# Two transformer blocks on one core: where the down factors of a hidden pair are split, and how the conditioning rows are summed

## The chip, the core and the metric

The kernel runs on one core of one Trainium2 chip. The metric is the device time of the whole program in microseconds (us). Three runs of the kernel before gave 2796.27, 2797.93 and 2798.13 us, median 2797.93.

The engines that matter: TensorE (PE in the profile; PEld is its weight load), VectorE (DVE), ScalarE (ACT), GpSimd (POOL) and SyncE (SP). ACT and SP also issue DMAs; those rows read ACTq and SPq.

## The reference

Two layers run one after the other on a 1024 x 1024 activation (1024 tokens, model width 1024), all in fp32. The first is a hybrid mixer (gated MLP, differential attention, top-k attention) with layer norm, the second is conditioned on a vector `c` and mixes by stick-breaking attention and pooling. Each ends in the same kind of feed-forward part with 2816 hidden units. What the change touches is this:

```python
# layer 1, feed-forward
gate, up = jnp.split(x @ w_gu, 2)                       # 2 x (1024 x 2816)
x = layer_norm(alpha * x + (silu(gate) * up) @ w_down)
# layer 2, conditioning rows (shift, gain and scale), 6 x 1024 numbers
mod = jax.nn.silu(c) @ w_cond + b_cond
# layer 2, feed-forward
f = (jax.nn.silu(h @ w_gate) * (h @ w_up)) @ w_down
```

## The kernel before

**Matmuls.** An fp32 product is made of three matmuls on rounded parts (`mm3`, lines 97 to 99): each operand is split into a high part, a cast by ACT to the type fp32r (`split`, line 80), and a low part, what the cast left over, by DVE (line 84). A matmul has 128 x 128 weights and 512 columns.

**Feed-forward parts** (called FFN1 and FFN2 here). The 22 hidden tiles are taken in 11 pairs by `gate_up`. Pairs 0 and 1 are multiplied directly. Each pair from 2 to 10 uses a Strassen-Winograd scheme: seven products for the gate and seven for up, in the order 1, 6, 2, 7, 5, 4, 3, each of 12 matmuls, so 168 to a pair. G7 stands here for gate product 7 and U3 for up product 3. In names of the trace the activation operand tells the product: B11 is 1, T2 is 6, B21 is 2, T3 is 7, T1 is 5, T4 or B12 is 4, B22 is 3; `x1` in front is FFN1, `x3` is FFN2.

`product` (line 940) takes a slot of the tag "w" (a `wst` tile), casts the weights' high part into it on ACT (line 945), makes the low part on DVE, or on POOL for products 2 and 4 (line 946), issues the matmuls and then adds the result up in `after`: line 958 copies product 1, 963 is product 6, 983 the silu of product 2 of the gate, 966 product 7, 968 product 5, 971 product 4, 976 product 3; line 985 is the silu of the other gate parts, 992 and 994 multiply gate and up (994 on POOL).

**Down factors.** A finished pair is four 128 x 512 quarters (a11, a12, a21, a22: two hidden tiles by two halves of the tokens). The down projection needs seven factors of them: A11, A12, A22, and four sums, S1 = a21 + a22, S3 = a11 - a21, S2 = S1 - a11, S4 = a12 - S2. `forms` (line 1034) is a generator that makes one factor a step: the sum on DVE (lines 1044, 1047, 1050, 1059), then `store`, which takes another slot of the tag "w" (an `hf` tile), splits into it and puts the 512 KB DMA to DRAM off until the next store (`flush`, line 1023, on ACT's queue). The last two pairs, 9 and 10, store four plain quarters instead. `wst` and `hf` tiles share six slots, so a cast may have to wait until the store of an earlier `hf` has landed.

Before the change `gate_up` makes `todo = forms(p, ...)` after all 14 products of pair p, and steps it once after each product of the next pair's gate.

**Conditioning.** `cond_steps(j)` (line 1260) makes conditioning row j of six during FFN1: for each of eight blocks of `w_cond`, a 512 KB load `raw_c` on SP's queue (line 1265) and one DVE operation that scales it and adds it to `mod` (1267, 1269), then the bias, a split with a two-matmul column sum per half (1284) and a gain. `extra1` steps it after every second product of a Strassen pair.

**Order.** The whole program is written in one stream; a scheduler of the framework then sets each engine's order from modelled times, and `soon()` (high priority) pulls splits and evictions forward. At run time each engine goes through its list in that order, and an instruction that waits holds up all behind it on that engine.

Of the kernel before, what the change touches and what calls it, by code (L numbers as in the profile page):

```python
# [9 lines left out]
F32 = mybir.dt.float32  # L10
# [6 lines left out]
OP = mybir.AluOpType  # L17
# [5 lines left out]
D = 1024  # L23
P = 128
NB = S // P
KT = D // P
# [12 lines left out]
def two_blocks(ctx: ExitStack, tc: tile.TileContext, a):  # L39
    nc = tc.nc  # L40
    V, A, T, G, DMA = nc.vector, nc.scalar, nc.tensor, nc.gpsimd, nc.sync
# [14 lines left out]
    def slot(tag, shape, dtype, name):  # L56
        return strm.tile(shape, dtype, tag=tag, bufs=SLOTS[tag], name=name)
# [57 lines left out]
    def row(t, src):  # L115
        DMA.dma_start(t, src.partition_broadcast(P))
        return t
# [22 lines left out]
    for i, (k0, nk) in enumerate(((0, 3), (3, 3), (6, 2))):  # L140
        h, l = load_split(a["wu0"][:, k0:k0 + nk, :], [P, nk, U0N], hi_eng="dve", lo_eng="pool")
# [66 lines left out]
    for h, l, k0, nk in wu0:  # L208
        for j in range(nk):
            k = k0 + j  # L210
# [258 lines left out]
    for blk in SCORED:  # L469
        L = (blk + 1) * P  # L470
        nch, n = key_chunks(L)
# [10 lines left out]
        for h in range(8):  # L482
# [3 lines left out]
            r = p1.tile([P, S], F32, name="r", **GT)  # L486
# [164 lines left out]
    accp, _ = pool("accp", "right")  # L651
# [249 lines left out]
    NPAIR = (NFT - NLAST) // 2  # L901
    FORMS = ("A11", "S3", "S2", "A22", "S1", "A12", "S4")
    h_d = [{n: dr.tile([P, 2, 512], F32, name=f"h_d{i}{n}") for n in FORMS} for i in range(NPAIR)]
    hl_d = [dr.tile([P, 2, S], F32, name=f"hl_d{i}") for i in range(NLAST)]
# [91 lines left out]
    class Ffn:  # L996
# [36 lines left out]

        def forms(self, i, b):

            if i >= NPAIR:
                for (j, th), x in b.items():
                    self.store(hl_d[2 * (i - NPAIR) + j][:, :, th * 512:(th + 1) * 512], x)
                    yield
                return  # L1040
            a11, a12, a21, a22 = b[0, 0], b[1, 0], b[0, 1], b[1, 1]
            put = lambda n, x: self.store(h_d[i][n], x)
            s1 = self.post("s1")
            V.tensor_tensor(s1, a21, a22, op=OP.add)
            put("A11", a11)
            yield
            V.tensor_tensor(a21, a11, a21, op=OP.subtract)  # L1047
            put("S3", a21)
            yield
            V.tensor_tensor(a11, s1, a11, op=OP.subtract)  # L1050
            put("S2", a11)
            yield
            put("A22", a22)
            yield
            put("S1", s1)
            yield
            put("A12", a12)
            yield
            V.tensor_tensor(a12, a12, a11, op=OP.subtract)
            put("S4", a12)  # L1060
            yield

        def gate_up(self, wg, wu, late, extra=None):


            act = self.act

            def direct(f, th, g, u):
                pg = ps_lg()
                for n, (wh, wl) in enumerate((g, u)):  # L1070
                    for k in range(KT):
                        mm3(pg[:, n, :], wh[:, k, :], wl[:, k, :], act.at(0, k, th), act.at(1, k, th), k == 0, k == KT - 1)
                s = self.post("silu")
                with soon():
                    A.activation(s, pg[:, 0, :], AF.Silu)
                    V.tensor_tensor(s, s, pg[:, 1, :], op=OP.mult)
                return s

            def load(w, f):
                return load_split(w(f), [P, KT, P])  # L1080

            wt = [self.w0, [load(wg, 1), load(wu, 1)], [load(wg, 2)], []]
            b = {}
            for th in range(2):
                for f in range(2):
                    b[f, th] = direct(f, th, *wt[f])
                    if th == 0:
                        late(4 + 2 * f)
                        late(5 + 2 * f)
            todo = self.forms(0, b)  # L1090
            wt[2].append(load(wu, 2))
            wt[3].append(load(wg, 3))
            b = {}
            for th in range(2):
                b[0, th] = direct(2, th, *wt[2])
            wt[3].append(load(wu, 3))
            for th in range(2):
                for _ in range(4):
                    next(todo, None)
                b[1, th] = direct(3, th, *wt[3])  # L1100
            act.sums()
            todo = self.forms(1, b)
            for p in range(2, NFT // 2):
                f = 2 * p
                ms = {}
                for m in range(2):
                    w = (wg, wu)[m]
                    ms[m] = (Gate, Up)[m]([self.load(w(f + i), [P, KT, P]) for i in range(2)], act, self.post)
                    if m == 1:
                        ms[1].gate = ms[0]  # L1110
                    for q in (1, 6, 2, 7, 5, 4, 3):
                        ms[m].product(q)
                        next(todo, None)
                        if extra is not None:
                            extra()
                todo = self.forms(p, {(i, l): ms[0].p[i, l] for i in range(2) for l in range(2)})
            for _ in todo:
                pass
            self.flush()
# [129 lines left out]
    fpool, f_done = pool("fpool")  # L1249


    sc = fpool.tile([P, KT], F32, name="sc")
# [6 lines left out]

    def cond_steps(j):  # L1260

        m = fpool.tile([P, D], F32, tag="rows", bufs=1, name="mod")
        for k in range(KT):
            r = slot("raw", [P, D], F32, "raw_c")
            DMA.dma_start(r, a["w_cond_2"][k * P:(k + 1) * P, j * D:(j + 1) * D])
            if k == 0:
                V.tensor_scalar_mul(m, r, sc[:, 0:1])
            else:
                V.scalar_tensor_tensor(m, r, sc[:, k:k + 1], m, op0=OP.mult, op1=OP.add)
            yield  # L1270

        b = slot("raw", [P, D], F32, "raw_b")
        DMA.dma_start(b[0:1, :], a["b_cond_2"][j * D:(j + 1) * D].partition_broadcast(1))
        V.tensor_tensor(m[0:1, :], m[0:1, :], b[0:1, :], op=OP.add)
        gn = {1: "g_mix_pre_2", 2: "g_mix_post_2", 4: "g_ffn_pre_2", 5: "g_ffn_post_2"}.get(j)
        if gn is not None:
            g = row(slot("raw", [P, D], F32, "raw_g"), a[gn])
        for c in range(2):
            cs = slice(c * 512, (c + 1) * 512)
            hl = [ffn1.post(f"m{i}", F32R) for i in "hl"]  # L1280
            split(*hl, m[:, cs])
            o = ps_mm(512)
            for i in range(2):
                T.matmul(o, ones, hl[i], start=i == 0, stop=i == 1)
            V.tensor_copy(m[:, cs], o)
            yield
        if gn is not None:
            V.scalar_tensor_tensor(m, m, 1.0 if j in (1, 4) else 0.0, g, op0=OP.add, op1=OP.mult)
        DMA.dma_start(mod_d[j:j + 1, :], m[0:1, :])

    n_extra = [0]
# [1 line left out]

    def extra1():
        n_extra[0] += 1
        if n_extra[0] % 2 == 0:
            next(conds, None)

    tail = {}
# [339 lines left out]
    n = 0  # L1639
# [121 lines left out]
```

## Time and profile before

| what | value |
|---|---|
| median of 3 runs | 2797.93 us |
| the profiled execution's own time | 2798.06 us |
| its span, first to last instruction | 2796.3 us |
| mean granted TensorE clock | 0.935 of full |
| PE busy | 2436.5 us, 87% of the span |
| DVE, ACT, POOL busy | 65%, 39%, 28% |
| the chain that ended last | PE 48%, DVE 9%, DMA 7%, ACT 5%, POOL 4% |

The span and the times stand 1.8 us apart. FFN1's pairs lie from about 747 to 1257 us, FFN2's from about 2094 to 2565 us. Where the granted clock is 0.5, TensorE runs at 1.2 GHz rather than 2.4 GHz.

### The profile page before, as it was taken

The numbers are of one execution on the slowest core, as the hardware profiler recorded it, in microseconds if no ns is written. First come the engines' busy times: TensorE is split into PE (matmuls) and PEld (weight loads), VectorE is DVE, ScalarE is ACT, GpSimd is POOL, SyncE is SP. The second block draws the span as 40 slices with busy tenths as digits, with TensorE's granted clock in tenths as the row PEclk, the third lists the DMA queues.
The fourth block names the chain that finished last, engine by engine and source line by source line (L and its number), as shares of the span: only waits on it lengthen the run. The fifth ranks groups of instructions, "written<-read, shape, count | busy, mean of one in ns | idle before, by whom it ended". The sixth has DMA issues, their size and how long they took to land.

```text
span 2796.3 us, 32919 instructions
## 1 busy us (share of the span) xinstructions
PE 2436.5 (87%) x11584; PEld 1990.3 (71%) x11584; DVE 1825.5 (65%) x3042; ACT 1099.3 (39%) x2013; POOL 778.0 (28%) x751
## 2 busy tenths in 40 slices
PE   8889987998988777889997989898697887888998
PEld 8878776886766556668876777687576665666886
DVE  4889788468666677658775366757645545545776
ACT  4558954333232233223235344445723323324221
POOL 2511234136311121120034043428531111112004
PEclk9989998999999898999998999899798998999999
DMA  4244545422444455467733424644233323327663
GB/s 171 66 140 121 147 132 172 111 87 93 158 150 149 151 188 167 163 236 254 264 129 115 150 89 127 198 114 148 97 113 131 110 91 123 118 91 260 237 228 133
DMA packets 171726, 414.02 MB, mean 148 GB/s; under 512 B 21788, under 2 KB 67868, under 8 KB 170536
## 3 DMA queue, kind: packets, MB, share of 16 engines
q1 hardware_dynamic: 149064, 337.45, 37.6%
q10 hardware_dynamic: 22496, 74.46, 6.6%
q8 instruction: 92, 1.51, 0.2%
q14 instruction: 74, 0.61, 0.1%
HBM read 278.65 MB, written 133.19 MB: 147 GB/s over the span
## 4 chain that ended last, share of the span: by engine, by line
PE 48%; DVE 9%; DMA 7%; ACT 5%; POOL 4%; issue 3%; SPq 0%; ACTq 0%; DVEq 0%; POOLq 0%
PE plg L97 8%; PE plg L98 7%; PE plg L99 7%; PE pmm L97 5%; PE pmm L99 5%; PE pmm L98 5%; PE ptr L97 2%; PE ptr L99 2%; PE ptr L98 2%; ACT hf L80 2%; DMA raw_c<-in_w_cond_dram 1%; ACT wst L945 1%; POOL u L994 1%; PE plg L337 1%; DMA hl_d<-hf 1%
## 5 line engine op out<-in xcount | busy, mean ns | idle before, releaser
L946 POOL TENSOR_TENSOR wst<-rw,wst 128x512 fp32r<-128x512 f32 x57 | 82.0, 1438 | 327.0 <-ACT wst L945 263.1
L337 PE MATMUL plg<-qk,qk 128*128 128x384 f32 (+4 forms) x480 | 127.1, 383 | 30.0 <-DVE mn L350 15.0
L84 POOL TENSOR_TENSOR wl<-raw,wh 128x1024 fp32r<-128x1024 f32 (+2 forms) x28 | 66.3, 2373 | 304.9 <-ACT wh L80 278.5
L946 DVE TENSOR_TENSOR wst<-tt,wst 128x512 fp32r<-128x512 f32 x144 | 110.3, 767 | 36.7 <-ACT wst L945 36.5
L80 ACT CAST hf<-u 128x512 fp32r<-128x512 f32 x36 | 22.2, 616 | 275.1 <-DVE u L1047 222.9
L994 POOL TENSOR_TENSOR u<-u,u 128x512 f32<-128x512 f32 x36 | 47.3, 1314 | 293.1 <-DVE u L968 243.7
L945 ACT CAST wst<-tt 128x512 fp32r<-128x512 f32 x144 | 88.6, 617 | 81.2 <-PE plg L99 28.0
L1562 DVE TENSOR_TENSOR_SCAN sab<-sab 128x640 f32<-128x640 f32 (+7 forms) x64 | 103.2, 1617 | 22.0 <-ACT sab L1560 21.3
L278 ACT ACTIVATE junk_a<-xi,cand 128x1024 bf16<-128x1024 f32 (+1 forms) x124 | 109.0, 879 | 12.5 <-DVE cand L267 6.9
L337 PEld LDWEIGHTS plg<-qk,qk 128*128 128x128 f32 x480 | 83.6, 201 | 40.6 <-DVE mn L350 16.4
L80 ACT CAST ws<-st 128x512 fp32r<-128x512 f32 x72 | 45.0, 628 | 124.9 <-PE plg L99 77.1
L1188 DVE TENSOR_TENSOR dacc<-dacc,plg 128x1024 f32<-128x1024 f32 x48 | 58.5, 1219 | 53.2 <-PE plg L99 53.2
L162 PE MATMUL pmm<-wh,xh 128*128 128x256 f32 (+1 forms) x320 | 91.7, 287 | 1.3 <-DVE stgl L399 0.8
L163 PE MATMUL pmm<-wl,xh 128*128 128x256 f32 (+1 forms) x320 | 91.0, 285 | 0.0
L164 PE MATMUL pmm<-wh,xl 128*128 128x256 f32 (+1 forms) x320 | 90.8, 284 | 0.0
L351 ACT ACTIVATE e<-e,mn 128x128 f32<-128x128 f32 (+7 forms) x96 | 74.2, 773 | 37.2 <-DVE mn L350 35.9
L945 ACT CAST wst<-rw 128x512 fp32r<-128x512 f32 x86 | 53.1, 617 | 89.4 <-PE plg L99 31.3
L97 PE MATMUL pmm<-xh,wh 128*128 128x512 f32 x192 | 77.2, 402 | 7.4 <-DVE oB L585 4.8
L692 PE MATMUL pmm<-woh,mixh 128*128 128x512 f32 x192 | 78.9, 411 | 4.8 <-ACT mixh L681 2.6
L80 ACT CAST wh<-raw 128x1024 fp32r<-128x1024 f32 x54 | 56.6, 1049 | 67.2 <-PE pmm L98 28.8
L976 DVE TENSOR_TENSOR u<-plg,u 128x512 f32<-128x512 f32 x36 | 24.9, 691 | 86.2 <-PE plg L99 86.1
L971 DVE TENSOR_TENSOR p<-plg,u 128x512 f32<-128x512 f32 x36 | 24.8, 690 | 84.3 <-PE plg L99 84.2
(733 smaller groups left out, 8565.3 us busy)
## 6 DMA issues: line engine op xcount, KB each, us to landing
raw_c<-in_w_cond_dram SPq DMA_DIRECT2D x48, 512.0 KB, 4.6
qk<-qkd SPq DMA_DIRECT2D x72, 256.0 KB, 6.9
rw<-in_wgu_dram SPq DMA_DIRECT2D x36, 512.0 KB, 4.0
rw<-in_w_down_dram SPq DMA_DIRECT2D x26, 512.0 KB, 4.8
x_d<-acc SPq DMA_DIRECT2D x24, 512.0 KB, 2.9
qk<-qk2d SPq DMA_DIRECT2D x48, 256.0 KB, 4.2
raw<-in_wqk_dram SPq DMA_DIRECT2D x20, 512.0 KB, 4.8
raw<-in_w_down_dram SPq DMA_DIRECT2D x18, 512.0 KB, 4.5
```

The costliest lines, as they stand in the source:

```text
L80: A.copy(hi, src)
L97: T.matmul(out, lh, rh, start=start, stop=False, skip_group_check=more)
L98: T.matmul(out, lh, rl, start=False, stop=False, skip_group_check=more)
L99: T.matmul(out, ll, rh, start=False, stop=stop, skip_group_check=more)
L162: T.matmul(o, at(0, k, tb * P, P), h[:, j, :], start=(k == 0), stop=False)
L163: T.matmul(o, at(0, k, tb * P, P), l[:, j, :], start=False, stop=False)
L164: T.matmul(o, at(1, k, tb * P, P), h[:, j, :], start=False, stop=(k == KT - 1))
L278: A.activation(junk_a[:, :L], xi[self.blks[i]], AF.Sign, bias=c, accum_out=self.cnt[:, i:i + 1])
L337: T.matmul(pl[:, c, :n], q[:, isl], k2[:, c * n:(c + 1) * n], start=(j == 0), stop=last)
L945: A.copy(wh, x)
L946: (G if p in (2, 4) else V).tensor_tensor(wl, x, wh.bitcast(F32), op=OP.subtract)
L1562: V.tensor_tensor_scan(sa[:, ::-1], sa[:, ::-1], sa[:, ::-1], 1.0, op0=OP.mult, op1=OP.bypass)
```

## The change

Three things change. `forms` is made when five up products of a pair are still to come (before U5, whose quarter is not finished then), not after the last, and yields its factors in another order: those that need no sum first (A11, A22, A12, stepped after U5, U3 and the next pair's G1), then the sums (S3, S2, S1, S4, after G2, G7, G5 and G4), with two empty steps between. The plain pairs get the same kind of order, and the direct pairs take six steps rather than four per half. `cond_steps` now uses each load one step after it was issued, so that it has 13 steps to a row and not 10. The diff:

```diff
@@ -1033,28 +1033,33 @@
 
         def forms(self, i, b):
 
+
             if i >= NPAIR:
-                for (j, th), x in b.items():
-                    self.store(hl_d[2 * (i - NPAIR) + j][:, :, th * 512:(th + 1) * 512], x)
+                plain = lambda j, th: self.store(hl_d[2 * (i - NPAIR) + j][:, :, th * 512:(th + 1) * 512], b[j, th])
+                for n in ((0, 0), None, (1, 1), (1, 0), None, (0, 1)):
+                    if n:
+                        plain(*n)
                     yield
                 return
+            put = lambda n, x: self.store(h_d[i][n], x)
+            put("A11", b[0, 0])
+            yield
+            yield
+            put("A22", b[1, 1])
+            yield
+            put("A12", b[1, 0])
+            yield
+            yield
             a11, a12, a21, a22 = b[0, 0], b[1, 0], b[0, 1], b[1, 1]
-            put = lambda n, x: self.store(h_d[i][n], x)
             s1 = self.post("s1")
             V.tensor_tensor(s1, a21, a22, op=OP.add)
-            put("A11", a11)
-            yield
             V.tensor_tensor(a21, a11, a21, op=OP.subtract)
             put("S3", a21)
             yield
             V.tensor_tensor(a11, s1, a11, op=OP.subtract)
             put("S2", a11)
             yield
-            put("A22", a22)
-            yield
             put("S1", s1)
-            yield
-            put("A12", a12)
             yield
             V.tensor_tensor(a12, a12, a11, op=OP.subtract)
             put("S4", a12)
@@ -1095,7 +1100,7 @@
                 b[0, th] = direct(2, th, *wt[2])
             wt[3].append(load(wu, 3))
             for th in range(2):
-                for _ in range(4):
+                for _ in range(6):
                     next(todo, None)
                 b[1, th] = direct(3, th, *wt[3])
             act.sums()
@@ -1109,11 +1114,14 @@
                     if m == 1:
                         ms[1].gate = ms[0]
                     for q in (1, 6, 2, 7, 5, 4, 3):
+                        if m == 1 and q == 5:
+                            for _ in todo:
+                                pass
+                            todo = self.forms(p, ms[0].p)
                         ms[m].product(q)
                         next(todo, None)
                         if extra is not None:
                             extra()
-                todo = self.forms(p, {(i, l): ms[0].p[i, l] for i in range(2) for l in range(2)})
             for _ in todo:
                 pass
             self.flush()
@@ -1259,22 +1267,25 @@
 
     def cond_steps(j):
 
-        m = fpool.tile([P, D], F32, tag="rows", bufs=1, name="mod")
-        for k in range(KT):
-            r = slot("raw", [P, D], F32, "raw_c")
-            DMA.dma_start(r, a["w_cond_2"][k * P:(k + 1) * P, j * D:(j + 1) * D])
-            if k == 0:
-                V.tensor_scalar_mul(m, r, sc[:, 0:1])
-            else:
-                V.scalar_tensor_tensor(m, r, sc[:, k:k + 1], m, op0=OP.mult, op1=OP.add)
+        m, last = fpool.tile([P, D], F32, tag="rows", bufs=1, name="mod"), None
+        for k in range(KT + 1):
+            if k < KT:
+                r = slot("raw", [P, D], F32, "raw_c")
+                DMA.dma_start(r, a["w_cond_2"][k * P:(k + 1) * P, j * D:(j + 1) * D])
+            if k == 1:
+                V.tensor_scalar_mul(m, last, sc[:, 0:1])
+            elif k:
+                V.scalar_tensor_tensor(m, last, sc[:, k - 1:k], m, op0=OP.mult, op1=OP.add)
+            last = r
             yield
 
         b = slot("raw", [P, D], F32, "raw_b")
         DMA.dma_start(b[0:1, :], a["b_cond_2"][j * D:(j + 1) * D].partition_broadcast(1))
-        V.tensor_tensor(m[0:1, :], m[0:1, :], b[0:1, :], op=OP.add)
         gn = {1: "g_mix_pre_2", 2: "g_mix_post_2", 4: "g_ffn_pre_2", 5: "g_ffn_post_2"}.get(j)
         if gn is not None:
             g = row(slot("raw", [P, D], F32, "raw_g"), a[gn])
+        yield
+        V.tensor_tensor(m[0:1, :], m[0:1, :], b[0:1, :], op=OP.add)
         for c in range(2):
             cs = slice(c * 512, (c + 1) * 512)
             hl = [ffn1.post(f"m{i}", F32R) for i in "hl"]
@@ -1286,6 +1297,7 @@
             yield
         if gn is not None:
             V.scalar_tensor_tensor(m, m, 1.0 if j in (1, 4) else 0.0, g, op0=OP.add, op1=OP.mult)
+        yield
         DMA.dma_start(mod_d[j:j + 1, :], m[0:1, :])
 
     n_extra = [0]
@@ -1293,7 +1305,7 @@
 
     def extra1():
         n_extra[0] += 1
-        if n_extra[0] % 2 == 0:
+        if n_extra[0] % 4:
             next(conds, None)
 
     tail = {}
```

`extra1` steps the conditioning on three of four products, no longer on one of two.

How the scheduler's order changes is shown at two places. The numbers behind the names are running numbers of the tiles.

First, PE at the boundary between pairs 4 and 5 of FFN2, in the kernel before: the first matmul of each stretch of a product (`wst` is its weights).

```order
L99 MATMUL plg_18199<-x3B22h_16355,wst_18253 128x512
L97 MATMUL pmm_18276<-x3B21h_16352,wst_18327 128x512
...
L97 MATMUL plg_18349<-x3T3h_17286,wst_18350 128x512
...
L99 MATMUL pmm_18276<-x3B21h_16352,wst_18327 128x512
...
L99 MATMUL plg_18349<-x3T3h_17286,wst_18350 128x512
...
L97 MATMUL plg_18349<-x3T1h_16701,wst_18373 128x512
...
L97 MATMUL pmm_18443<-x3B11h_16350,wst_18444 128x512
```

The same place in the changed kernel:

```order
L99 MATMUL plg_18199<-x3B22h_16355,wst_18257 128x512
L97 MATMUL ptr_18306<-x3T2h_17293,wst_18307 128x512
...
L97 MATMUL pmm_18284<-x3B21h_16352,wst_18328 128x512
...
L97 MATMUL plg_18352<-x3T3h_17286,wst_18353 128x512
...
L97 MATMUL pmm_18443<-x3B11h_16350,wst_18444 128x512
...
L97 MATMUL plg_18352<-x3T1h_16701,wst_18377 128x512
...
L99 MATMUL pmm_18443<-x3B11h_16350,wst_18444 128x512
```

G6 (`x3T2`) now stands between U3 (`x3B22`) and G2 (`x3B21`), and before it stood ahead of U3; U1 (`x3B11`) has begun ahead of G5 (`x3T1`).

ACT there, before: `hf` casts are factors (u2 is S3, s11 is S2, u3 is A22, s1 is S1, p1 is A12), `wst` casts are weights (in order G2, G7, G5, G4), L1023 issues a store, L983 is the silu of G2.

```order
L80 CAST hf_18324<-u2_18020 128x512
L945 CAST wst_18327<-raw_18272 128x512
L80 CAST hf_18346<-s11_18042 128x512
L945 CAST wst_18350<-tt_18351 128x512
L80 CAST hf_18370<-u3_18067 128x512
L945 CAST wst_18373<-tt_18302 128x512
L1023 DMA h_d4S3_6143<-hf_18324 128x1024
L1023 DMA h_d4S2_6144<-hf_18346 128x1024
L1023 DMA h_d4A22_6145<-hf_18370 128x1024
L80 CAST hf_18391<-s1_18294 128x512
...
L945 CAST wst_18394<-rw_18274 128x512
L983 ACTIVATE s11_18342<-pmm_18276 128x512
```

ACT there in the changed kernel (the `hf` of u2 is S3, of s11 S2, of s1 S1 and of p1 S4; the `wst` rows are G2, G7, G5, G4 and last U1):

```order
L945 CAST wst_18328<-raw_18280 128x512
...
L983 ACTIVATE s11_18343<-pmm_18284 128x512
L80 CAST hf_18349<-u2_18026 128x512
L945 CAST wst_18353<-tt_18354 128x512
L80 CAST hf_18374<-s11_18043 128x512
L945 CAST wst_18377<-tt_18308 128x512
L80 CAST hf_18395<-s1_18345 128x512
L945 CAST wst_18398<-rw_18282 128x512
L1023 DMA h_d4S3_6143<-hf_18349 128x1024
L1023 DMA h_d4S2_6144<-hf_18374 128x1024
L80 CAST hf_18417<-p1_18000 128x512
...
L945 CAST wst_18444<-rw_18439 128x512
```

S3's cast stood directly ahead of G2's weight cast; now it stands behind the silu of G2 and ahead of G7's weight cast, and the stores of S3 and S2 are issued behind G4's cast and ahead of S4's.

Second, DVE in FFN1, where a block of conditioning steps lies. Before, around the end of pair 4 (L971 and L976 add up U4 and U3, L963 the next G6, L966, L968 U7, U5):

```order
L1288 SCALAR_TENSOR_TENSOR mod_7921<-mod_7921,raw_g_8287 128x1024
L1267 TENSOR_SCALAR mod_8380<-raw_c_8381,sc_6740 128x1024
L1269 SCALAR_TENSOR_TENSOR mod_8380<-raw_c_8439,sc_6740,mod_8380 128x1024
L971 TENSOR_TENSOR p1_8241<-plg_8297,u2_8266 128x512
L1269 SCALAR_TENSOR_TENSOR mod_8380<-raw_c_8488,sc_6740,mod_8380 128x1024
L1269 SCALAR_TENSOR_TENSOR mod_8380<-raw_c_8533,sc_6740,mod_8380 128x1024
L1269 SCALAR_TENSOR_TENSOR mod_8380<-raw_c_8582,sc_6740,mod_8380 128x1024
L976 TENSOR_TENSOR u2_8266<-plg_8297,u2_8266 128x512
L1269 SCALAR_TENSOR_TENSOR mod_8380<-raw_c_8623,sc_6740,mod_8380 128x1024
L1269 SCALAR_TENSOR_TENSOR mod_8380<-raw_c_8663,sc_6740,mod_8380 128x1024
L1044 TENSOR_TENSOR s1_8406<-u2_8093,u3_8143 128x512
```

In the changed kernel, a block within the up products of pair 4 (L992 multiplies U2, L84 splits a factor, L946 a weight):

```order
L963 TENSOR_TENSOR u2_8292<-ptr_8272,p1_8270 128x512
L1276 TENSOR_SCALAR mod_8247<-raw_c_8248,sc_6740 128x1024
L1278 SCALAR_TENSOR_TENSOR mod_8247<-raw_c_8294,sc_6740,mod_8247 128x1024
L971 TENSOR_TENSOR p1_8084<-plg_8150,u2_8111 128x512
L1278 SCALAR_TENSOR_TENSOR mod_8247<-raw_c_8313,sc_6740,mod_8247 128x1024
L1278 SCALAR_TENSOR_TENSOR mod_8247<-raw_c_8336,sc_6740,mod_8247 128x1024
L992 TENSOR_TENSOR s11_8132<-s11_8132,pmm_8254 128x512
L1278 SCALAR_TENSOR_TENSOR mod_8247<-raw_c_8377,sc_6740,mod_8247 128x1024
L84 TENSOR_TENSOR hf_8357<-s11_8132,hf_8357 128x512
L966 TENSOR_TENSOR u3_8334<-plg_8316,u2_8292 128x512
L1278 SCALAR_TENSOR_TENSOR mod_8247<-raw_c_8403,sc_6740,mod_8247 128x1024
```

The eight steps of a block stay close together on DVE; this block moved from the pair's end to among the evictions of up products and the splits between them.

## Rows read from the trace of the kernel before

**Rows 1.** Sections 1 and 4 of the page: busy time; the chain that ended last.
```profile
PE 2436.5 (87%) x11584; PEld 1990.3 (71%) x11584; DVE 1825.5 (65%) x3042; ACT 1099.3 (39%) x2013; POOL 778.0 (28%) x751
...
PE 48%; DVE 9%; DMA 7%; ACT 5%; POOL 4%; issue 3%; SPq 0%; ACTq 0%; DVEq 0%; POOLq 0%
```

**Rows 2.** Busy per window: length, PE, PEld, DVE, ACT, POOL; PEclk, DMA share, GB/s.
```profile
2154.69:2470.03 315.34, 260.92 (x1009) 202.25 (x1009) 165.77 (x241) 90.98 (x163) 55.86 (x42) 0.91 0.31 110
2224.00:2250.00 26.00, 26.00 (x113) 21.01 (x112) 11.51 (x16) 6.21 (x12) 3.71 (x3) 1.00 0.18 61
2260.00:2264.30 4.30, 4.28 (x10) 3.07 (x11) 3.95 (x7) 2.66 (x5) 1.28 (x1) 0.51 0.65 211
2271.40:2274.50 3.10, 3.08 (x7) 2.47 (x8) 1.68 (x3) 0.78 (x2) 0.00 (x0) 0.50 0.98 390
911.00:929.00 18.00, 5.47 (x22) 3.85 (x21) 15.49 (x15) 1.14 (x2) 2.88 (x3) 0.73 0.71 217
```

**Rows 3.** PE's waits, 2150 to 2475 us: us in total, times, longest.
```profile
PE pmm L97 <- ACT wst L945: 37.0, 7, 5.3
...
PE plg L97 <- ACT hf L80: 18.0, 6, 3.5
...
PE plg L97 <- DVE p L971: 4.7, 6, 0.8
```

**Rows 4.** Timeline, pair 4 to 5 in FFN2: start, us, engine; in brackets idle before.
```profile
2254.77 0.69 DVE L976 TENSOR_TENSOR u<-plg,u 128x512 f32<-128x512 f32 x1 [3.15 <-PE plg L99]
2255.61 1.26 POOL L994 TENSOR_TENSOR u<-u,u 128x512 f32<-128x512 f32 x1 [2.55 <-DVE u L976]
...
2258.11 0.68 DVE L1047 TENSOR_TENSOR u<-s,u 128x512 f32<-128x512 f32 x1
2258.83 0.62 ACT L80 CAST hf<-u 128x512 fp32r<-128x512 f32 x1 [15.67 <-DVE u L1047]
...
2259.35 0.61 ACT L945 CAST wst<-raw 128x512 fp32r<-128x512 f32 x1
...
2260.02 0.79 PE L97 MATMUL pmm<-x3B21h,wst 128*128 128x512 f32 x1 [5.29 <-ACT wst L945]
...
2261.90 0.33 ACTq L1023 DMA_DIRECT2D h_d4S<-hf  x1
...
2266.95 0.62 ACT L945 CAST wst<-rw 128x512 fp32r<-128x512 f32 x1 [2.86 <-DMA h_d4S<-hf]
2267.48 0.59 ACT L983 ACTIVATE s<-pmm 128x512 f32<-128x512 f32 x1
...
2271.42 0.77 PE L97 MATMUL plg<-x3T1h,wst 128*128 128x512 f32 x1 [3.53 <-ACT hf L80]
```

**Rows 5.** DMA issues, 2260.1 to 2260.3 us, then 2261.85 to 2261.95: KB, us to landing.
```profile
h_d4S<-hf ACTq DMA_DIRECT2D x1, 512.0 KB, 2.7
...
h_d4S<-hf ACTq DMA_DIRECT2D x1, 512.0 KB, 5.0
```

**Rows 6.** PE's waits, 2090 to 2570 us.
```profile
PE pmm L97 <- ACT wst L945: 40.7, 9, 5.3
...
PE plg L97 <- ACT ws L80: 4.4, 1, 4.4
```

**Rows 7.** PE's waits in FFN1, 800 to 1210 us.
```profile
PE pmm L97 <- ACT wst L945: 44.9, 10, 11.6
...
PE plg L97 <- DVE p L971: 9.4, 8, 4.0
...
PE pmm L1284 <- DVE ml L84: 7.8, 2, 3.9
```

**Rows 8.** The conditioning's DVE line, its waits, and the landing of its loads.
```profile
L1269 DVE SCALAR_TENSOR_TENSOR mod<-raw_c,sc,mod x42: 1269/1284/2227, 711.8 to 1181.3; 128x1024 f32<-128x1024 f32 x42
...
  DMA raw_c<-in_w_cond_dram: 13.3, 14
...
raw_c<-in_w_cond_dram SPq DMA_DIRECT2D x48, 512.0 KB, 4.6
```

## The prediction, made before the changed kernel ran

> **What bounds the kernel now.** I read sections 1 and 4 of the page first: TensorE is busy for 87% of the span, but only 48% of the chain that ended last is TensorE's; DVE, DMA, ACT and POOL share 25% of it [rows 1]. So the time lies in places where TensorE waits for them. Next came the windows: FFN2's six regular pairs take 315.34 us, 52.56 each, in which TensorE is busy for 260.92 [rows 2]. The waits then say for what: per pair one wait of about 5.3 us (37.0 in 7) for a weight cast on ACT, one of 3.0 (18.0 in 6) for a factor's cast on ACT, one of 0.8 for an addition on DVE [rows 3]. Last came the timeline at one boundary, which shows who holds whom [rows 4].
>
> The first wait. U3's result is added on DVE at 2254.77 (0.69), multiplied on POOL (1.26), subtracted on DVE (S3's sum, until 2258.79), and cast on ACT from 2258.83. G2's weight cast stands behind S3's cast on ACT and starts at 2259.35, though its operand is an untouched weight; TensorE starts at 2260.02, 5.29 us late.
>
> The second wait. G4's cast needs a slot that S2 holds until its store has landed: issued at 2261.90, landed 2266.93. ACT stands still for 2.86 us, with the silu of G2 and the cast of S4 behind it; the addition of G7's result on DVE, which T1 (G5) has to wait for, comes late too, and T1 starts at 2271.42, 3.53 us late.
>
> Each wait has an aftermath. After the first the granted clock is 0.51: 10 matmuls take 4.30 us, after the second 0.50, 7 take 3.10 [rows 2]. These are 1.2 of 2.4 GHz. In an undisturbed stretch 113 matmuls take 26.00 us, 0.23 each. The slow stretches thus cost 4.30 - 2.30 = 2.0 and 3.10 - 1.61 = 1.5 us.
>
> The pair's account: 168 x 0.23 = 38.6; waits 5.3 + 3.0 + 0.8 = 9.1; slow clock 3.5; the remaining 1.4 are small gaps and records missing, which I leave as they are.
>
> **The change part by part.**
>
> *Order of the factors, seven boundaries in each FFN.* S3's cast now stands behind G2's, and between U3 and G2 TensorE has G6, 12 x 0.23 = 2.8 us of work. That the long sum of U3 is not in G2's way any more removes the first wait: 5.3 us. What is late next is G7 and, behind it, U1. I walk from the end E of G2, with durations as in rows 4 (ACT's casts start about 0.52 apart, as 2258.83 and 2259.35 do): silu of G2 to E+0.7, S3's cast to E+1.2, G7's weight cast to E+1.8, where G7 can begin: 1.8 us of wait. G7's low part on DVE stands behind S3's low part and some sums (0.69 each) and ends near E+3.2; with the first matmuls on the high part, about 1.0 more is lost within G7. ACT goes on: casts of S2, G5, S1, G4 to E+3.9; the stores of S3 and S2 stand behind these and are issued near E+3.6 and E+4.0 (an `hf` is stored when the next factor is made). S4's cast needs S3's slot, 2.7 us after the issue (rows 5, the store alone): E+6.4 to 7.0. G3's cast needs S2's slot, whose store lands behind S3's, near E+7.6: to E+8.2. U1's cast follows: E+8.8. TensorE starts U1 at E+8.9, and G5 stands behind U1's first matmuls though its cast is long done. Of these 8.9 us G7 fills 2.8: 6.1 us are waited, in pieces of 1.8, 1.0 and 3.3. At U5, whose sum now gates the bank of U4, I expect the 0.8 that the same addition costs at U4 and U3 today, and 0.3 at G1's low part. Waits after: 7.2, against 9.1. Slow clock: only the last piece, 3.3, is near a wait that shows a slow stretch behind it (3.53, which cost 1.5), so 1.5 against 3.5. The pair is 38.6 + 7.2 + 1.5 + 1.4 = 48.7, which is 3.9 less. Bounds: if S2 lands 2.7 after its own issue, the waited part is 5.2, and without any slow stretch the pair saves 5.3 + 3.0 + 0.8 + 3.5 - 6.3 = 6.3; if S3 and S2 each take 4.4 to 5.0 as S2 does today [rows 5], it is 7.5, with slow stretches of 2.0 it saves 12.6 - 8.6 - 2.0 = 2.0. Fourteen such boundaries in two FFNs: 14 x 3.9 = 54.6 (28 to 88).
>
> *Ends of the FFNs.* Two further waits of the first kind (40.7 - 37.0 = 3.7) and 4.4 at the start of the down projection [rows 6]. The plain stores are cast beside the last up products now. I take 3.5 of the first and 1.0 of the second, since the last quarter's cast and store still stand between U3 and the down projection: 4.5 in each FFN, 9 in all (0 to 16).
>
> *Direct pairs, six steps per half rather than four.* The factors are the same number of casts, beside direct products that run to several us each; no wait of theirs is in the rows. Zero, with 3 us to either side.
>
> *Conditioning in FFN1.* The work is the same: 48 loads, 48 DVE steps of 1.28 us [rows 8], 13 steps to a row at three of four products, so 6 x 13 / 0.75 = 104 products or 7.4 pairs rather than 120 or 8.6. A load is now issued one step ahead of its use, which would hide part of the 4.6 us to landing; but the order shows that the eight steps stay a block on DVE, so DVE still waits for loads (today 13.3 us in 14 times). What is new is the place. Before, the worst block sat at a pair's end, with TensorE busy for 5.47 of 18.00 us there [rows 2] and an 11.6 us wait [rows 7]; others cost TensorE little. Now five blocks lie beside up products or G7 to U1, where DVE's additions free the banks. I let each block delay TensorE by two of its steps more than before: 5 x 2 x 1.28 = 12.8 us lost (0 if DVE's idle time takes them, 25 if it is four steps).
>
> *Sum:* 54.6 + 9 - 12.8 = 50.8 us gained against the profiled execution's 2798.06: 2747.3. That execution lies 0.13 above the median of the runs, which changes nothing.
>
> A rule to weigh here: the Trainium skill, DMA: Bandwidth & Descriptors, section "Issuing engines are not separate DMA queues", says that DMAs of the scalar and the sync engine run on the same 16 engines and interleave. The trace agrees: S3's store took 2.7 us, and S2's, issued when a weight load and S3 were under way, 5.0. By it S3's store too would be late when a load meets it, which is the third rival.
>
> **The rivals.**
>
> *The waits cost no clock.* The pieces 1.8, 1.0 and 3.3 are each shorter than any wait that shows a slow stretch behind it here (3.53 is the shortest). Then 1.5 more is saved at each of 14 boundaries, 21 us: 2726. Against it: 3.3 is close to 3.53. The Trainium skill (TensorE: Matmul & The Clock Gate, "HAM oscillation") has the same direction: it says that the clock falls when TensorE's idle gaps between bursts are long, and each return is paid again; that the three pieces stay below it is shown by no run here.
>
> *The stores land late.* S3's and S2's landing decide when U1 begins. If both take some 4.4 to 5.0 us, U1 is 1.4 later at each boundary: 20 us, 2767. For it: S2's 5.0 [rows 5]. Against it: the walk has the two stores issued together, with fewer others in the queue at that time.
>
> *Slower: conditioning blocks stop TensorE.* DVE works in order; while a step waits for a load, the eviction behind it waits and the bank of the next product with it. The block at 911 to 929 left TensorE 18.00 - 5.47 = 12.5 us idle [rows 2]. If each of five blocks costs that and one whole landing of 4.6 [rows 8] more, 17.1, the loss is 86 against 63.6 gained elsewhere: about 2820. It decides from 63.6 / 5 = 12.7 us a block. Against it: the four other blocks of today cost far less (the waits for DVE in FFN1 are 9.4 and 7.8 in all [rows 7]), and loads are issued a step earlier.
>
> *No change.* Either blocks at about 12.7 us, or the time merely moves from the first wait to the one before U1, with S2 and S3 landing late and both slow stretches kept: 2798.
>
> **How the numbers follow.** Forecast 0.62 at 2747; no clock lost 0.12 at 2726; late stores 0.12 at 2767; slower 0.08 at 2820; no change 0.06 at 2798. About 0.2%, 5.6 us, is what a measurement of this kernel can tell from no change. Faster is 0.62 + 0.12 + 0.12 = 0.86, same 0.06, slower 0.08. The range reaches from 2705 (the clock case with the ends of FFN gained in full and no loss by conditioning) to 2788 (late stores with a loss of 25 us by conditioning and a little more); slower and no change are left out, 0.14, and some 0.05 below.
>
> **What would show it.** The wait of 5.3 us before x3B21 gone in seven boundaries of FFN2; a wait before G7's first matmul of about 1.8, and before U1 in the gate of about 3.3, with ACT held by landing stores ahead of S4's and G3's casts; the regular pairs at 48 to 49 us (46.3 to 50.6) rather than 52.56. In FFN1 the pairs with a conditioning block 2 to 3 us longer than those without. Wrong would be: a wait of 5 us or more still before G2; U1 later than E+10; pairs with blocks over 12 us longer than others.

## The result, and the profile after

The changed kernel takes 2734.23 us (median of four runs, 2729.37 to 2739.02) against 2798.03: a ratio of 0.977, with an interval of 0.975 to 0.979. That is 63.8 us less; 50.8 were forecast. The profiled execution is the shortest of the four, 2729.37 us with a span of 2727.6, so in the two profiles the difference is 68.7 us.

By stages (first matmul of a stage to its last, read from the timelines): up to the end of FFN1's last up product 29.0 us are gained, in FFN2's gate and up 39.8, and elsewhere the two profiles agree within 1 us (725.6 after against 726.3 before between the FFNs, 225.4 against 224.8 from FFN2's last up product to the last matmul).

Sections 1 and 4 of the page after, answering to [rows 1]:

```profile
PE 2419.6 (89%) x11584; PEld 1977.9 (73%) x11584; DVE 1840.7 (67%) x3042; ACT 1099.3 (40%) x2013; POOL 784.8 (29%) x751
...
PE 51%; DVE 10%; DMA 5%; POOL 4%; issue 3%; ACT 3%; SPq 0%; ACTq 0%; DVEq 0%; POOLq 0%
```

The work is the same; in the chain that ended last DMA, ACT and DVE together fall from 21% to 18%.

TensorE's waits after, 2117 to 2457 us, the stretch that answers to [rows 3]:

```profile
PE plg L97 <- ACT wst L945: 12.0, 7, 1.7
PE pmm L97 <- ACT wst L945: 11.7, 6, 3.1
PE plg L97 <- DVE u L968: 6.1, 7, 0.9
PE plg L99 <- DVE wst L946: 4.7, 7, 0.7
PE plg L97 <- ACT u L985: 2.2, 2, 1.2
PE plg L97 <- DVE u L966: 1.2, 1, 1.2
```

The 5.3 us wait of seven pairs is gone. In its place stand, at seven boundaries, 1.7 before G7, 0.7 within G7 (line L99, a low part), 1.1 to 3.1 before U1 (`pmm`, at six; at the seventh G5 comes first and waits 1.2 for an addition, L966), and 0.9 at U4.

The timeline of the changed kernel between pairs 5 and 6 of FFN2, answering to [rows 4]:

```profile
2255.37 0.62 ACT L945 CAST wst<-rw 128x512 fp32r<-128x512 f32 x1
...
2263.39 0.60 ACT L983 ACTIVATE s<-pmm 128x512 f32<-128x512 f32 x1 [6.93 <-PE pmm L99]
2263.89 0.61 ACT L80 CAST hf<-u 128x512 fp32r<-128x512 f32 x1
2264.40 0.62 ACT L945 CAST wst<-tt 128x512 fp32r<-128x512 f32 x1
...
2264.92 0.62 ACT L80 CAST hf<-s 128x512 fp32r<-128x512 f32 x1
...
2265.07 0.50 PE L97 MATMUL plg<-x3T3h,wst 128*128 128x512 f32 x1 [1.71 <-ACT wst L945]
...
2265.25 0.33 ACTq L1023 DMA_DIRECT2D h_d5S<-hf  x1
...
2265.44 0.62 ACT L945 CAST wst<-tt 128x512 fp32r<-128x512 f32 x1
...
2267.17 1.61 POOL L946 TENSOR_TENSOR wst<-raw,wst 128x512 fp32r<-128x512 f32 x1 [7.24 <-ACT wst L945]
...
2267.55 1.79 DVE L925 TENSOR_TENSOR tt<-tt,raw 128x512 f32<-128x512 f32 x1
...
2267.88 0.62 ACT L80 CAST hf<-p 128x512 fp32r<-128x512 f32 x1 [0.79 <-DMA h_d5S<-hf]
...
2270.34 0.62 ACT L945 CAST wst<-tt 128x512 fp32r<-128x512 f32 x1 [1.83 <-DVE hf L84]
...
2271.54 0.62 ACT L945 CAST wst<-raw 128x512 fp32r<-128x512 f32 x1 [0.58 <-DVE hf L84]
2272.21 0.79 PE L97 MATMUL pmm<-x3B11h,wst 128*128 128x512 f32 x1 [3.14 <-ACT wst L945]
```

ACT stands still for 6.93 us at the silu of G2 with S3's cast and G7's weight cast behind it. G2 ends at 2263.36; G7 starts 1.71 later; U1 starts 8.85 after G2's end. On the way G3's cast waits 1.83 for a low part on DVE: the store of S1 is issued by ACT, waits for that low part, and the cast is behind the store.

Windows after (columns as in [rows 2]): five pairs, from the start of one G7 to that of a later one; then the ten matmuls behind G7's 0.7 us wait at two boundaries; then the stretch behind U1's start at a third:

```profile
2171.01:2410.80 239.79, 211.78 (x840) 163.08 (x840) 142.29 (x201) 76.41 (x136) 47.24 (x35) 0.95 0.33 121
2172.42:2176.40 3.98, 3.98 (x10) 2.97 (x10) 3.98 (x6) 1.37 (x4) 1.60 (x1) 0.57 0.71 254
2266.48:2269.10 2.62, 2.59 (x10) 1.80 (x10) 2.62 (x3) 1.24 (x3) 1.61 (x1) 1.00 0.80 328
2321.10:2326.00 4.90, 4.90 (x13) 3.79 (x12) 1.73 (x3) 1.24 (x2) 1.28 (x1) 0.50 0.25 92
```

A pair takes 239.79 / 5 = 47.96 us, against 52.56 before. Each of the seven boundaries still has a slow stretch. At five it begins in G7 itself (clock 0.57, ten matmuls in 3.98 us; the wait behind it, for U1 or G5, is then 1.1 to 1.6), and at the last two of these the clock is slow again, or still, behind U1's start. At the other two it lies behind U1's 3.1 us wait (0.50).

### The profile page after: what moved, and what is told of

Read it like the earlier page. It is cut to its first block, busy times and chain, and to the rows that moved or that the text cites. A ratio compares the mean times of both kernels' runs of the same rounds, so it can differ in the third digit from the quotient of the medians.

```text
span 2727.6 us, 32854 instructions
## 1 busy us (share of the span) xinstructions
PE 2419.6 (89%) x11584; PEld 1977.9 (73%) x11584; DVE 1840.7 (67%) x3042; ACT 1099.3 (40%) x2013; POOL 784.8 (29%) x751
## 4 chain that ended last, share of the span: by engine, by line
PE 51%; DVE 10%; DMA 5%; POOL 4%; issue 3%; ACT 3%; SPq 0%; ACTq 0%; DVEq 0%; POOLq 0%
PE plg L97 8%; PE plg L98 7%; PE plg L99 7%; PE pmm L97 6%; PE pmm L98 5%; PE pmm L99 5%; PE ptr L99 2%; PE ptr L97 2%; PE ptr L98 2%; DMA raw_c<-in_w_cond_dram 1%; DVE hf L84 1%; DVE wst L946 1%; DVE tt L925 1%; PE plg L337 1%; DVE mod L1278 1%
## 5 line engine op out<-in xcount | busy, mean ns | idle before, releaser
L946 POOL TENSOR_TENSOR wst<-rw,wst 128x512 fp32r<-128x512 f32 x57 | 90.0, 1578 | 406.6 <-ACT wst L945 323.9
L84 POOL TENSOR_TENSOR wl<-raw,wh 128x1024 fp32r<-128x1024 f32 (+2 forms) x28 | 66.1, 2367 | 306.4 <-ACT wh L80 280.1
L946 DVE TENSOR_TENSOR wst<-tt,wst 128x512 fp32r<-128x512 f32 x144 | 118.5, 826 | 23.7 <-ACT wst L945 23.6
L1196 DVE TENSOR_TENSOR dacc<-dacc,plg 128x1024 f32<-128x1024 f32 x48 | 58.5, 1220 | 55.8 <-PE plg L99 55.8
L98 PE MATMUL pmm<-xl,wh 128*128 128x512 f32 x192 | 77.3, 403 | 0.0
L99 PE MATMUL pmm<-xh,wl 128*128 128x512 f32 x192 | 77.2, 402 | 0.0
L693 PE MATMUL pmm<-wol,mixh 128*128 128x512 f32 x192 | 76.3, 397 | 0.0
L694 PE MATMUL pmm<-woh,mixl 128*128 128x512 f32 x192 | 75.8, 399 | 0.3 <-DVE mixl L84 0.3
```

Of the source, the lines that this page charges most:

```text
L84: eng.tensor_tensor(lo, src, hi.bitcast(F32), op=OP.subtract)
L98: T.matmul(out, lh, rl, start=False, stop=False, skip_group_check=more)
L99: T.matmul(out, ll, rh, start=False, stop=stop, skip_group_check=more)
L946: (G if p in (2, 4) else V).tensor_tensor(wl, x, wh.bitcast(F32), op=OP.subtract)
```

## The experiments

Ratios are against the kernel before, run beside each.

**e1, the factors alone.** The changed kernel with `cond_steps` and its pace as before:

```diff
-        if n_extra[0] % 4:
+        if n_extra[0] % 2 == 0:
```

and the ten-step `cond_steps`.

> The changed kernel with the conditioning steps and their pace as before. My theory: the factors' order makes the whole gain, and the new place of the conditioning costs a little of it. Between the ends of U3 of pairs 2 and 10 the profiles show 443.6 us in FFN1 against 411.4 in FFN2 before (32 more, with conditioning), and 415.4 against 375.4 after (40 more): so about 8 us faster than the changed kernel, some 2726 us. Rival: the lagged steps are themselves a gain, since a load has a step more to land; then this is slower than the changed kernel, 2745 or more.

Measured: 2733.16 us, 0.977 [0.975, 0.980], the same as the changed kernel: neither the 2726 of the theory nor the 2745 of the rival. In the profile FFN1 ends 8.6 us sooner than in the changed kernel (1215.0 against 1223.6), as expected, but the two spans, 2728.4 and 2727.6, do not show it. The change to the factors, their start and their order together, makes the whole gain; the small cost of the conditioning's place isn't settled by these runs.

**e2, the conditioning alone.** The kernel before with the lagged steps at three of four products.

> The kernel before with the lagged conditioning steps and their faster pace alone. My theory: no gain, 0 to 15 us slower than before (about 2806), since the blocks move among evictions. Rival: a gain of 10 us or more (below 2788), because DVE waits less for loads. FFN2 must be as before in either case (52.6 us a pair).

Measured: 2796.75 us, 0.999 [0.998, 1.001]. No change, neither a gain of 10 us nor a loss. FFN2's wait of 5.3 us is there as before, 2150 to 2475 us:

```profile
PE pmm L97 <- ACT wst L945: 35.3, 7, 5.3
```

In its profile FFN1 ends 10.1 us sooner than before (1242.6 against 1252.6), and the rest takes 9 us more.

**e3, the order without the early start.**

```diff
-                        if m == 1 and q == 5:
-                            for _ in todo:
-                                pass
-                            todo = self.forms(p, ms[0].p)
...
+                for _ in todo:
+                    pass
+                todo = self.forms(p, ms[0].p)
```

A11, A22, A12 are thereby made after G1, G2, G7 of the next pair, and S3, S2, S1, S4 after G4, G3, U1, U6.

> The changed kernel, but the factors of a pair are begun after its last product as before: only their order is new (A11, A22, A12, then the sums, with the empty steps between; what is left when the up products end is done there). My theory: what counts is that S3's cast, with U3's long chain ahead of it, no longer stands before G2's weight cast; so the 5.3 us wait is gone here too and the time is within 15 us of the changed kernel's, 2720 to 2750. Rival: what counts is that part of the splitting lies beside the last up products; then most of the gain is gone, 2775 or more.

Measured: 2630.76 us, 0.941 [0.939, 0.943]. Both expectations missed: it is 103 us faster than the changed kernel. The page of windows over six pairs of FFN2, and TensorE's waits, 2040 to 2470 us:

```profile
2115.20:2364.60 249.40, 238.49 (x1010) 187.34 (x1009) 168.72 (x241) 92.21 (x162) 57.62 (x42) 1.00 0.38 139
```

```profile
PE plg L97 <- DVE u L968: 12.2, 9, 1.5
...
PE ptr L97 <- ACT wst L945: 2.1, 7, 0.3
```

41.57 us a pair, at full clock: of the 52.56 all of the waits but 1.8 us, and all of the slow clock, are gone. e3 differs from the changed kernel in two things, the late start and the later sums; the next runs were to tell which of them does it.

**e4, the early start with the sums one step later.**

```diff
             put("A12", b[1, 0])
             yield
             yield
+            yield
```

> The changed kernel with the four sums one step later (S3 after G7 rather than after G2). The two waits at G7 (1.71 and 0.67 us) go, since G7's cast now stands ahead of G2's silu and of S3's cast. My theory: the chain S3, S2, S1, S4 and then U1's cast sets the next start, 8.5 to 8.9 us after G2, whatever G7 does; so the wait before U1 grows by what G7 gains and the time is the same, 2725 to 2745. Rival: the 2.4 us are gained at each of 16 boundaries: 38 us, 2696.

Measured: 2772.09 us, 0.991 [0.989, 0.993]: 38 us slower than the changed kernel, the sign of neither expectation. The timeline of e4 after G7's end in FFN2:

```profile
2184.99 0.69 DVE L966 TENSOR_TENSOR u<-plg,u 128x512 f32<-128x512 f32 x1 [4.83 <-PE plg L99]
2185.60 0.68 DVE L1056 TENSOR_TENSOR s<-u,u 128x512 f32<-128x512 f32 x1
2186.31 0.69 DVE L1057 TENSOR_TENSOR u<-s,u 128x512 f32<-128x512 f32 x1
2187.04 0.62 ACT L80 CAST hf<-u 128x512 fp32r<-128x512 f32 x1 [3.77 <-DVE u L1057]
...
2187.56 0.61 ACT L945 CAST wst<-tt 128x512 fp32r<-128x512 f32 x1
...
2188.23 0.50 PE L97 MATMUL plg<-x3T1h,wst 128*128 128x512 f32 x1 [3.28 <-ACT wst L945]
```

G7's own waits are gone, as planned, but G5's weight cast now stands behind S3's. The sums stand on DVE behind the addition of G7, which can begin only when G7 has ended. So G5 waits for addition, two sums and two casts, 3.28 us, and U1 again for 2.6 to 3.3, and every boundary has slow clock behind these waits. Behind G2 there was no such addition on DVE: only the silu of G2 was in the way.

**e5, the early start with the sums where e3 has them.** Three more empty steps rather than one.

> The changed kernel, factors begun beside the last up products as there, but the four sums three steps later: S3 after G4, S2 after G3, S1 after U1, S4 after U6, the places they have in e3. My theory, formed after e3 and e4: what TensorE waits for is the run of sums (DVE sum, ACT cast, DVE low part, store) put straight behind G2, since ACT then has the silu of G2 and S3's cast ahead of the next weight casts; where the plain factors are split hardly matters. Then this is near e3: 2620 to 2665. Rival: starting early is what costs (tiles of A22 and A12 hold slots across the pair's end): 2700 or more.

Measured: 2664.03 us, 0.952 [0.950, 0.954], inside the first expectation. TensorE's waits, 2117 to 2385 us (six pairs):

```profile
PE plg L97 <- DVE u L966: 15.9, 12, 1.8
PE plg L97 <- DVE u L968: 6.7, 12, 0.9
...
PE pmm L97 <- ACT wst L945: 2.5, 6, 0.4
```

The waits for casts are gone but for 0.4 a pair; what is left are waits for additions, up to 1.8 us at product 5 (L966) and up to 0.9 at product 4 (L968). At 44.6 us a pair it stands 3.0 behind e3, and the last pair takes 39.5 us against 32.4: splitting A11 and A22 beside the last up products is no gain but a small loss, 33 us in the whole.

**e6, the late start with the sums close behind.** e3 without its empty steps: S3 after G7, as in e4.

> The other corner: factors begun after the pair as in e3, but with no empty steps, so that S3, S2, S1, S4 come after G7, G5, G4, G3 (S3 where e4 has it). By the same theory G5 waits for a weight cast behind S3's, as in e4, and U1 for the stores: 2745 to 2785. Rival (the late start makes e3's gain): 2620 to 2665.

Measured: 2766.86 us, 0.988 [0.986, 0.990], as the theory had it. TensorE's waits before U1 (`pmm`) and G5, 2135 to 2440 us:

```profile
PE pmm L97 <- ACT wst L945: 19.7, 6, 3.4
PE plg L97 <- ACT wst L945: 19.7, 6, 3.3
```

The two starts lie within 6 us of each other where S3 comes after G7 (e4, e6), and 33 apart where it comes after G4 (e5, e3); the place of the sums moves the time by 108 to 136 us.

**e7, the stores on SP.**

```diff
-                A.dma_start(dst, src)
+                DMA.dma_start(dst, src)
```

> The changed kernel with the factors' stores issued by SP and not by ACT. In its profile G3's and U1's weight casts on ACT waited 1.83 and 0.58 us until a low part on DVE was done: a store that ACT issues waits for that low part, and the casts behind it wait too. My theory: without the stores on ACT, U1 starts about 2 us sooner, some 30 us over 16 boundaries: 2695 to 2715. Rival: the slots, free only when a store has landed, hold U1 as before: 2725 to 2745, or later, where stores stand behind weight loads on SP.

Measured: 2741.67 us, 0.979 [0.976, 0.981]: no gain, my theory fell, and the time lies where the rival had it. The timeline of e7 at a boundary of FFN2, where G2 ended at about 2221.18:

```profile
2223.07 2.13 SPq L1023 DMA_DIRECT2D h_d4S<-hf  x2
...
2226.95 0.62 ACT L80 CAST hf<-p 128x512 fp32r<-128x512 f32 x1 [2.03 <-DMA h_d4S<-hf]
...
2228.14 0.62 ACT L945 CAST wst<-tt 128x512 fp32r<-128x512 f32 x1 [0.58 <-DMA h_d4S<-hf]
2228.66 0.61 ACT L945 CAST wst<-rw 128x512 fp32r<-128x512 f32 x1
...
2229.33 0.80 PE L97 MATMUL pmm<-x3B11h,wst 128*128 128x512 f32 x1 [2.43 <-ACT wst L945]
```

The 1.83 us wait for a low part is gone, but the casts of S4 and G3 now wait 2.03 and 0.58 us for the slots of S3 and S2 to land. U1 starts 8.15 us after G2, only 0.7 sooner (7.6 to 8.8 at the seven boundaries). Two holds of nearly the same length lay over each other, and to take one away uncovers the other. A pair of FFN2 gains 0.4 us by it (47.6 against 48.0), while FFN1 ends 10.8 us later in e7's profile; why was not looked into.

**e8, e3 with the old conditioning.**

> e3 with the conditioning steps and their pace as before. In e1 and e2 the conditioning part moved the time by less than 0.3%; my theory is that this holds here too: within 10 us of e3, 2621 to 2641. Rival: with TensorE's other waits gone, DVE's blocks in FFN1 show, and the lagged steps are worth 10 us or more: above 2641.

Measured: 2624.79 us, 0.938 [0.936, 0.940], within the 10 us, with an interval that overlaps e3's. The lagged steps gain nothing that shows.

**e9, the kernel before with empty steps.**

```diff
             put("A11", a11)
-            yield
+            for _ in range(5):
+                yield
```

> The kernel before, with its own order of factors (A11, S3, S2, A22, S1, A12, S4), its late start and its conditioning; only five empty steps stand behind A11, so that S3 comes after G4 rather than G6 (and six steps per half in the direct pairs, so that the factors are done). My theory: where S3 is cast against the next pair's products is all that counts; the rest of the order does nothing: 2615 to 2660, a pair of FFN2 41 to 43 us. Rival: the plain factors must come first, or start early, for the waits to go: 2700 or more.

Measured: 2707.19 us, 0.967 [0.965, 0.969], and 45.6 to 46.9 us for each of the pairs 3 to 8 of FFN2: my theory missed, and the time lies in the rival's range. One long wait a boundary is left (the `plg` row, 2040 to 2470 us), and the timeline of e9 behind a U3 shows what it is for:

```profile
PE plg L97 <- ACT hf L80: 33.2, 7, 4.7
```

```profile
2241.96 0.69 DVE L976 TENSOR_TENSOR u<-plg,u 128x512 f32<-128x512 f32 x1 [4.66 <-PE plg L99]
2242.73 1.26 POOL L994 TENSOR_TENSOR u<-u,u 128x512 f32<-128x512 f32 x1 [4.06 <-DVE u L976]
2244.02 0.69 DVE L1044 TENSOR_TENSOR s<-u,u 128x512 f32<-128x512 f32 x1 [1.37 <-POOL u L994]
2244.63 0.68 DVE L963 TENSOR_TENSOR u<-ptr,p 128x512 f32<-128x512 f32 x1
2245.23 0.68 DVE L1048 TENSOR_TENSOR u<-s,u 128x512 f32<-128x512 f32 x1
2245.83 0.68 DVE L966 TENSOR_TENSOR u<-plg,u 128x512 f32<-128x512 f32 x1
...
2246.66 0.69 PE L97 MATMUL plg<-x3T1h,wst 128*128 128x512 f32 x1 [4.74 <-ACT hf L80]
```

S1's sum (L1044) is still in A11's step, though S1 is stored much later. DVE waits there for POOL's multiplication of U3, and the additions of G6 and G7 (L963, L966) wait behind it, and G5 for the latter. The named releaser, an ACT cast that began 0.66 us earlier, is put down by time; the addition L966 at 2245.83 fits as well, and e11 tells.

**e10, e8 with the sums one step later still** (S3 after G3).

> e8 with the four sums one more step later (S3 after G3, S2 after U1, S1 after U6, S4 after U2). My theory: at S3 after G4 only 1.5 us of wait a pair are left in FFN2, for an addition on DVE (line 968); the sums are already out of the way, so nothing more is gained: 2615 to 2635. Rival: the wait of 1.5 us goes too: 16 x 1.5 = 24 us, about 2601.

Measured: 2614.38 us, 0.934 [0.932, 0.936], the fastest of all. Its waits, 2040 to 2470 us:

```profile
PE plg L97 <- DVE u L968: 7.9, 9, 0.9
```

The wait for the addition L968 falls from 1.5 to 0.9, and the pair from 41.6 to 41.0 us. The time is just below the first expectation's low end; the whole 1.5 is not gained.

**e11, e9 with S1's sum later as well.**

```diff
-            s1 = self.post("s1")
-            V.tensor_tensor(s1, a21, a22, op=OP.add)
             put("A11", a11)
             for _ in range(5):
                 yield
+            s1 = self.post("s1")
+            V.tensor_tensor(s1, a21, a22, op=OP.add)
```

> e9 with S1's sum moved behind the five empty steps as well. In e9's profile one wait of 4.74 us was left at each boundary: S1's sum, still in the step of A11, waits on DVE for U3's multiplication on POOL, and the additions of G6 and G7, which G5 waits for, stand behind it. My theory: with that sum out of the way too, the kernel before, in its own order of factors and with its own late start, loses all its waits: 2615 to 2640, 41 to 42 us a pair of FFN2. Rival: the plain factors have to stand ahead of the sums, or start early, for that: 2690 or more.

Measured: 2649.11 us, 0.945 [0.943, 0.948], 9 us above the range. Six pairs of FFN2 take 41.0 us each, as expected:

```profile
2087.30:2333.30 246.00, 238.61 (x1010) 187.39 (x1009) 163.47 (x240) 92.98 (x162) 63.65 (x42) 1.00 0.39 141
```

e9's wait of 4.7 us is gone with S1's sum, so that sum was its cause, and e9's rival is refuted too. The order of the factors among themselves thus costs a regular pair nothing: with all sums late, the old order reaches what e10 reaches. In FFN2 the rest is at the last two pairs, which keep the old order of the plain quarters (36.3 and 42.8 us between the ends of their U3, against 41.0 and 32.4 in e10), 5.7 us, and FFN1, which ends 26.6 us later than in e10, holds the larger part; what of FFN1 belongs to which edit was not tried.

## Why the prediction was right

**The first wait.** Right in cause and size: S3's cast ahead of G2's weight cast held TensorE for 5.3 us; with it behind G2's, and G6 as cover, the wait is gone at all seven boundaries.

**What comes next.** The walk gave G7 1.8 us after G2, 1.0 more within it, and U1 8.9 after G2's end. Measured: 1.71, 0.67, and 8.83 to 8.85 at five boundaries, 8.49 at a sixth; at the seventh G5 went first, at E+8.5, and U1 followed at E+11.4. The time of U1 was right, but one step of the walk wasn't: I had S3 and S2 issued at E+3.6 and E+4.0, and their landing as the only hold. S2's store went out at E+3.7, but S3's at E+1.9, between S2's cast and G5's, at every boundary: the listing of ACT's order in the section on the change, from which I took E+3.6, has it behind G4's cast, and there the traces differ from it. [rows 5] had the sign of it, S3's store issued by 2260.3, where the listing of the kernel before puts it behind G5's cast (2261.43). At the boundary shown S3's landing held S4's cast for only 0.79; the longer hold was a store on ACT that waited for a low part on DVE, itself behind a subtraction of 1.79 us (L925, elsewhere 0.68). So it was at three of the seven boundaries; at three others a landing held G3's cast (0.60 to 2.43 us), and at the last the profile names G7's end. e7 showed that without the wait for the low part the landings hold U1 to within 0.7 us of the same start. That U1's time came out so close is in part luck: a hold that the walk did not have was about as long as the one it had.

**Waits and clock.** The sum had 7.2 us of waits and 38.6 + 1.5 + 1.4 = 41.5 of work for a pair of 48.7; measured was 47.96, with TensorE idle for (239.79 - 211.78) / 5 = 5.6 and busy for 42.4. Two terms were off, in opposite directions: the waits by 1.6, and the slow clock by about 0.9, because G7 ran slow at five of seven boundaries, where I had no slow stretch. They belong together: where G7 itself runs slow, it fills time that TensorE would have spent waiting for U1, since U1's start is set by ACT and DVE. The saving a pair is 4.6 and not 3.9.

**A term priced at nothing.** Pair 2 has a boundary of the same kind, with the factors of the directly multiplied pair 1 in its gate. I priced the direct stage's steps at 0 and left this boundary out; in FFN2 pair 2 gained 5.1 us (55.8 to 50.7) and the direct stage lost 1.3 (114.7 to 116.0). The last boundary with its end gained 3.7 of the 4.5 taken. The seven regular pairs gained 32.4, where the sum had 27.3; FFN2 in all gained 39.8, where it had 27.3 + 4.5 = 31.8.

**FFN1.** The sum had 31.8 - 12.8 = 19.0; measured 29.0, which is 10.8 less than FFN2. So the boundaries were underpriced here too. Whether the loss by conditioning had the right size is open: 10.8 and the 8.6 of e1's profile are near the 12.8 taken, but by their times the new steps do nothing that these runs resolve (e2: 0.999; e1 and the changed kernel 1 us apart), and in e2's profile they end FFN1 sooner. The sign named for it came out larger: pairs 3 to 8, which hold the blocks, took 49.9 to 57.3 us and pair 9, which holds none, 49.7, so up to 7.6 more and not 2 to 3. TensorE's longest waits in FFN1, 800 to 1210 us, answering to [rows 7]:

```profile
PE plg L97 <- ACT wst L945: 14.4, 5, 5.0
PE pmm L97 <- ACT wst L945: 13.1, 3, 6.6
PE plg L97 <- DVE u L966: 10.1, 5, 3.4
PE plg L97 <- DVE u L968: 9.8, 7, 3.7
```

The 11.6 us wait is gone; several of 3 to 7 stand in its place.

**The rivals.** That the pieces cost no clock is refuted by the windows above: every boundary keeps a slow stretch. Late stores (the second rival of the list; the prediction once calls it the third) came at single boundaries and did not make U1 late: at one S3's store landed only about 4.1 us after its issue and held S4's cast for 2.32, and U1 still began at E+8.83. Of the 142 stores of factors and quarters the trace shows the landing of 16, which took 2.6 to 8.5 us, 2.7 in the median. The slower case was wrong in its price: FFN1's longest pair took 57.3 us, 7.6 above the one without a block, so no block cost near 12.7 us more.

What the forecast did not see: far more was to be had from the sums' place, and in these runs the early start gains nothing. With the place held, the late start was 5 us faster (e6 against e4) and 33 (e3 against e5); with the start held, the place moved the time by 108 and 136. Each place has its own hold: after G6 S3's cast stands ahead of G2's (the kernel before, 2798); after G2 the silu and S3's cast stand ahead of G7's (2734, run with the early start alone); after G7 an addition, two sums and S3's cast stand ahead of G5's (2772, 2767); after G4 or G3 the next product's weights are already cast (2631, 2614 with the late start; 2664 with the early one, 2649 in the old order with S1's sum late too).

## What to carry to other kernels

In this kernel side work on an engine that goes through its list in order was cheap only where the casts for the next product were already ahead of it, and what it reads had long been written; look at what stands behind its first and its last instruction on each engine, not at its sum of time. A sum that is made early and used late (S1 in e9) can hold the evictions behind it while the engine seems idle. Where two holds end at nearly the same time, expect nothing from removing one; and test the placement itself, one step earlier and one later, since the time need not change in one direction.

## What the hardware showed that was not expected

Two short waits of 1.71 and 0.67 us with two matmuls between them were followed by ten matmuls at a granted clock of 0.57, near 1.2 GHz, at the boundary shown, and the clock fell within G7 at four more; at two boundaries with the same two waits ten matmuls ran at 1.00. The prediction had held that only a wait near 3.5 us does that. What tells the two cases apart is not shown. And a DVE subtraction of two 128x512 operands that took 0.68 us elsewhere took 1.79 where a POOL subtraction ran beside it (1.61 rather than 1.28), in the changed kernel and in e7 (1.78 and 1.61) alike. Of line 925's 92 operations in the changed kernel with nothing on POOL beside them none took more than 0.69 us.
